# Permuted column orders for thirteen of the sixteen input tiles of a decoder step

## The chip, the cores and the metric

The kernel runs on one core of a Trainium2 chip. The metric is the device time of one execution in microseconds (us). Two versions of the kernel are told of here, before and after one change; what is known at this point is the time and the profile of the version before.

## The reference

One inference step of a one-layer decoder trunk, for a prompt of 256 positions and 8 sample rows that share the weights. With `rmsnorm` the root-mean-square norm over the 2048 channels, and cut to what carries the work:

```
h = h + 0.5 * swiglu_ffn(rmsnorm(h, g1), ffn1_w_gate, ffn1_w_up, ffn1_w_down)    # 2048 -> 5504 -> 2048
z = rmsnorm(h, gm) @ w_in                                                       # 2048 -> 10528 columns
zp, zr, zq, zg = split(z)          # pooling | RWKV-7 r,k,v and low-rank | queries | 3 gates of 2048
merged = sigmoid(zg0) * pool(zp) + sigmoid(zg1) * rwkv7(zr) + sigmoid(zg2) * attend(zq, memory)
h = h + merged @ w_o
h = h + 0.5 * swiglu_ffn(rmsnorm(h, g2), ffn2_w_gate, ffn2_w_up, ffn2_w_down)
y = rmsnorm(h, gf)
```

Beside `y` the step returns the memory keys and values and the new recurrent, shift and pooling states. Everything is float32.

## The kernel before, in words

All activations stand transposed in SBUF: channels on the 128 partitions, the 264 positions (256 of the prompt and 8 sample rows, `NT`) along the free dimension. A vector of 2048 channels is thus sixteen tiles of 128x264, numbered k = 0 to 15 (`KD` = 16).

Float32 products are made of three matmuls each in the type fp32r. Every weight tile and every activation tile is split into a high part and a low part (`whi`, `wlo` for weights, `x4h`, `x4l` for input tile 4), and `mm3` (lines 227 to 230) adds high times high (L228), low activation times high weight (L229) and high activation times low weight (L230) into one PSUM accumulator. In each of these matmuls the weight block of 128x128 is the stationary operand, and the activation tile of 128x264 is the moving operand, read column by column; the accumulator takes 264 columns.

`proj` (lines 232 to 241) makes one projection: it runs over the sixteen (or 8, or 43) activation tiles and issues `mm3` for each, so a projection from the normalised input is 48 matmuls in a row into one accumulator. Of the projections, 255 read the sixteen normalised input tiles `x0` to `x15`: 86 gates and ups in each of the two feed-forward blocks (the first pair of the first block is made by `first_tiles`, lines 442 to 462), and 83 column blocks of `w_in`. The others read the feed-forward's hidden tiles (`g0` to `g42`, the down projections), the merged branches (`mg`, for `w_o`) and the outputs of the branches.

Weights are streamed once. `nxt` and `emit_load` (lines 172 to 225) fetch 512 KB at a time by a DMA on SP's queue, ScalarE (ACT) rounds it to the high part (L182), VectorE (DVE) subtracts for the low part (L184), up to two loads ahead of the matmuls; a load serves 24 matmuls.

The input tiles are made at three places, each time into the same sixteen pairs of buffers: `x_tile` (lines 397 to 409) from the loaded input, `norm_tile` (lines 274 to 276) at the end of the first feed-forward block, and `norm_tile` again after `w_o`. `split_into` (lines 256 to 263) writes the high part by ACT (L261) and the low part by DVE (L262). Each buffer is 264 floats, 1,056 bytes a partition, and the 32 buffers lie one behind the other in the order x0h, x0l, x1h, x1l and so on. The start of an input tile therefore moves on by 2,112 bytes from k to k+1, and four tiles make 8,448 bytes, which is 33 times 256.

The order of the work is set by the program text and by the framework's scheduler, which arranges instructions of each engine once, when the program is built.

Of the kernel before, what the change touches and what calls it, by code (L numbers as in the profile page):

```python
# [10 lines left out]
F32R = mybir.dt.float32r  # L11
# [4 lines left out]
P = 128  # L16
# [3 lines left out]
NT = SEQ + NB  # L20
FF = 5504
NF = FF // P
KD = D // P
# [16 lines left out]
GATE_AHEAD = 3  # L40
FIRST = ((0, 2), (2, 4), (4, 8), (8, 12), (12, 16))
MEM_AT = 6
MEM_END = 8


@with_exitstack
def step_kernel(ctx: ExitStack, tc: tile.TileContext, I, O):
# [8 lines left out]
    xp = ctx.enter_context(tc.tile_pool(name="xp", bufs=1))  # L56
# [10 lines left out]
    def sb(pool, shape, tag, dt=F32, bufs=None):  # L67
        kw = {} if bufs is None else {"bufs": bufs}
        return pool.tile(shape, dt, tag=tag, name=nm(tag), **kw)
# [157 lines left out]
    def mm3(out, wh, wl, xh, xl, first, last):  # L227
        PE.matmul(out, lhsT=wh, rhs=xh, start=first, stop=False)  # L228
        PE.matmul(out, lhsT=wh, rhs=xl, start=False, stop=False)  # L229
        PE.matmul(out, lhsT=wl, rhs=xh, start=False, stop=last)  # L230

    def proj(name, nk, xs, m=P):
        acc = acc_tile()
        k = 0
        while k < nk:
            wh, wl, n = nxt(name)
            for j in range(n):
                xh, xl = xs[k]
                mm3(acc[:m, :NT], wh[:, j, :], wl[:, j, :], xh, xl, k == 0, k == nk - 1)
                k += 1  # L240
        return acc


    nstate = {}
# [5 lines left out]
    def split(dst_pool, src, tag, scale=None, shape=(P, NT)):  # L250
        hi = sb(dst_pool, list(shape), tag + "h", F32R)
        lo = sb(dst_pool, list(shape), tag + "l", F32R)
        split_into(hi, lo, src, scale)
        return hi, lo
# [17 lines left out]
            POOL.tensor_tensor(out=sq, in0=sq, in1=t, op=ALU.add)  # L272

    def norm_tile(ht, d, gcol):
        nstate["xs"].append(split(xp, ht, f"x{d}", gcol))
        sq_acc(ht, d)

    def refine(r, x, t):
# [60 lines left out]
    g1v = sb(cst, [P, 16], "g1v")  # L339
    p = ps()  # L340
# [15 lines left out]
    r, gi, off = 0, 0, 0  # L356
    for name, n in vrows:
        if name == "rwkv_mu":
            gi, r, off = 1, 0, gsz[0]
# [35 lines left out]
    h = []  # L395
    norm_begin()

    def x_tile(j):
        p = ps()
        for i in range(2):  # L400
            PE.transpose(p[:, i * P:(i + 1) * P], xv[i][:, j * P:(j + 1) * P], ident)
        PE.transpose(p[:, SEQ:NT], xsm[:, j * P:(j + 1) * P], ident[:NB, :NB])
        ht = sb(hp, [P, NT], f"h{j}")
        hi = sb(xp, [P, NT], f"x{j}h", F32R)
        lo = sb(xp, [P, NT], f"x{j}l", F32R)
        split_into(hi, lo, p[:, :NT], g1v[:, j:j + 1])
        (ACT.copy if j % 4 == 3 else DVE.tensor_copy)(out=ht, in_=p[:, :NT])
        nstate["xs"].append((hi, lo))
        h.append(ht)

    xsq = sb(st, [P, 11], "xsq")
# [32 lines left out]
    def first_tiles():  # L444
        x_tile(0)
        x_tile(1)
        accs = [acc_tile(), acc_tile()]
        state["look"] = 0
        for c, (k0, k1) in enumerate(FIRST):
            wh, wl, n = nxt(("ffn1", "gu", 0))  # L450
            if c + 1 < len(FIRST):
                x_load(c + 1)
            state["look"] = 1 if c + 1 < len(FIRST) else 2
            for k in range(k0, k1):
                if k + 2 < KD:
                    x_tile(k + 2)
                xh, xl = nstate["xs"][k]
                for q in range(2):
                    qs = slice(q * P, (q + 1) * P)
                    mm3(accs[q][:, :NT], wh[:, k - k0, qs], wl[:, k - k0, qs], xh, xl, k == 0, k == KD - 1)  # L460
            x_squares(c)
        return accs

# [118 lines left out]
    xs, rstd = nstate["xs"], sb(xp, [P, NT], "rstd")  # L582
# [13 lines left out]
    xs, rstd = norm_end()  # L596
# [41 lines left out]
    for g in range(4):  # L638
        w = WIN[g]
        acc = proj(("zp", g), KD, xs)  # L640
# [764 lines left out]
```

## Time and profile before

| | before |
|---|---|
| median of 3 runs | 2436.65 us (2435.9 to 2442.38) |
| the profiled execution | 2439.21 us, its span 2437.5 us |
| TensorE matmul busy | 2391.9 us, 98% of the span |
| VectorE, ScalarE, GpSimd busy | 60%, 45%, 21% |
| mean granted TensorE clock | 0.988 of full speed |

The span runs from the first to the last instruction; the profiled execution's own time is 1.7 us longer. [...] Where the granted clock is 1.00 TensorE runs at 2.4 GHz, where it is 0.50 at 1.2 GHz.

### The profile page before, as it was taken

The numbers are of one execution on the slowest core, as the hardware profiler recorded it, in microseconds if no ns is written. First come the engines' busy times: TensorE is split into PE (matmuls) and PEld (weight loads), VectorE is DVE, ScalarE is ACT, GpSimd is POOL, SyncE is SP. The second block draws the span as 40 slices with busy tenths as digits, with TensorE's granted clock in tenths as the row PEclk, the third lists the DMA queues.
The fourth block names the chain that finished last, engine by engine and source line by source line (L and its number), as shares of the span: only waits on it lengthen the run. The fifth ranks groups of instructions, "written<-read, shape, count | busy, mean of one in ns | idle before, by whom it ended". The sixth has DMA issues, their size and how long they took to land.

```text
span 2437.5 us, 47572 instructions
## 1 busy us (share of the span) xinstructions
PE 2391.9 (98%) x19703; PEld 2347.7 (96%) x19703; DVE 1452.6 (60%) x1828; ACT 1086.6 (45%) x1440; POOL 514.6 (21%) x594
## 2 busy tenths in 40 slices
PE   8999999999999998999989999999999999999998
PEld 8899999999999998899979999999999999999998
DVE  5655555555545559898895765566555555544444
ACT  6444444444444445564323744444444444444444
POOL 2211111211000026462381210111211112210000
PEclk9999999999999999999899999999999999999999
DMA  8576666666666877777755677776666666666664
GB/s 234 157 217 181 182 179 179 180 181 176 191 187 186 233 185 216 211 187 190 194 173 162 169 187 196 209 200 178 181 180 179 179 181 181 179 174 174 175 184 129
DMA packets 822460, 452.03 MB, mean 185 GB/s; under 512 B 29092, under 2 KB 806982, under 8 KB 821963
## 3 DMA queue, kind: packets, MB, share of 16 engines
q1 hardware_dynamic: 821795, 448.91, 65.9%
q8 instruction: 154, 2.52, 0.4%
q14 instruction: 63, 0.52, 0.1%
q0 software_dynamic: 448, 0.08, 0.0%
HBM read 430.19 MB, written 18.96 MB: 184 GB/s over the span
## 4 chain that ended last, share of the span: by engine, by line
PE 92%; DMA 2%; DVE 2%; issue 1%; POOL 1%; ACT 1%; SPq 0%; DVEq 0%; POOLq 0%; ACTq 0%
PE acc L228 29%; PE acc L230 29%; PE acc L229 28%; DMA qb<-qs_d 1%; DVE wlo L184 1%; POOL kc L746 1%; PE acc L517 1%; PE acc L518 1%; PE acc L519 1%; DMA c4k<-AR_d 1%; PE ps L917 0%; DMA raw<-in_ffn_w_up_dram 0%; PE ps L1075 0%; DVE c4k L994 0%; PE ps L1024 0%
## 5 line engine op out<-in xcount | busy, mean ns | idle before, releaser
L184 DVE TENSOR_TENSOR wlo<-raw,whi 128x1024 fp32r<-128x1024 f32 (+2 forms) x783 | 970.9, 1240 | 728.2 <-ACT whi L182 673.3
L182 ACT ACTIVATE whi<-raw 128x1024 fp32r<-128x1024 f32 (+2 forms) x783 | 809.8, 1034 | 1121.6 <-PE acc L229 732.4
L549 POOL TENSOR_TENSOR t<-t,rstd 128x264 f32<-128x264 f32 x86 | 123.3, 1434 | 860.6 <-ACT s L548 848.5
L272 POOL TENSOR_TENSOR sqs<-sqs,sqt 128x264 f32<-128x264 f32 x44 | 42.2, 958 | 546.3 <-ACT sqt L271 546.3
L230 PE MATMUL acc<-x0h,wlo 128*128 128x264 f32 (+1 forms) x255 | 73.3, 288 | 8.5 <-DVE wlo L184 4.6
L228 PE MATMUL acc<-x0h,whi 128*128 128x264 f32 (+1 forms) x255 | 77.5, 304 | 0.0
L228 PE MATMUL acc<-x8h,whi 128*128 128x264 f32 (+1 forms) x255 | 76.3, 300 | 0.0
L228 PE MATMUL acc<-x4h,whi 128*128 128x264 f32 (+1 forms) x255 | 74.0, 291 | 1.5 <-ACT x4h L261 1.5
L230 PE MATMUL acc<-x8h,wlo 128*128 128x264 f32 (+1 forms) x255 | 72.6, 285 | 2.5 <-DVE wlo L184 2.5
L552 DVE TENSOR_TENSOR g<-acc,s 128x264 f32<-128x264 f32 x86 | 37.2, 432 | 63.2 <-PE acc L230 61.0
L230 PE MATMUL acc<-x5h,wlo 128*128 128x264 f32 (+1 forms) x255 | 74.0, 290 | 0.0
L229 PE MATMUL acc<-x5l,whi 128*128 128x264 f32 (+1 forms) x255 | 73.9, 290 | 0.0
L230 PE MATMUL acc<-x13h,wlo 128*128 128x264 f32 (+1 forms) x255 | 73.9, 290 | 0.0
L229 PE MATMUL acc<-x2l,whi 128*128 128x264 f32 (+1 forms) x255 | 73.8, 289 | 0.0
L229 PE MATMUL acc<-x1l,whi 128*128 128x264 f32 (+1 forms) x255 | 73.7, 289 | 0.0
L230 PE MATMUL acc<-x1h,wlo 128*128 128x264 f32 (+1 forms) x255 | 73.7, 289 | 0.0
L230 PE MATMUL acc<-x9h,wlo 128*128 128x264 f32 (+1 forms) x255 | 73.6, 289 | 0.0
L228 PE MATMUL acc<-x11h,whi 128*128 128x264 f32 (+1 forms) x255 | 73.6, 289 | 0.0
L228 PE MATMUL acc<-x3h,whi 128*128 128x264 f32 (+1 forms) x255 | 73.5, 289 | 0.0
L229 PE MATMUL acc<-x13l,whi 128*128 128x264 f32 (+1 forms) x255 | 73.5, 288 | 0.0
L230 PE MATMUL acc<-x6h,wlo 128*128 128x264 f32 (+1 forms) x255 | 73.4, 288 | 0.0
L230 PE MATMUL acc<-x2h,wlo 128*128 128x264 f32 (+1 forms) x255 | 73.4, 288 | 0.0
(1172 smaller groups left out, 8826.0 us busy)
## 6 DMA issues: line engine op xcount, KB each, us to landing
raw<-in_ffn_w_gate_dram SPq DMA_DIRECT2D x170, 512.0 KB
raw<-in_ffn_w_up_dram SPq DMA_DIRECT2D x170, 512.0 KB
raw<-in_w_in_dram SPq DMA_DIRECT2D x164, 512.0 KB
raw<-in_ffn_w_down_dram SPq DMA_DIRECT2D x160, 512.0 KB
raw<-in_w_o_dram SPq DMA_DIRECT2D x32, 512.0 KB
raw<-in_rwkv_out_dram SPq DMA_DIRECT2D x16, 512.0 KB
raw<-in_ffn_w_down_dram SPq DMA_DIRECT2D x32, 192.0 KB
raw<-in_w_mem_k_dram SPq DMA_DIRECT2D x8, 512.0 KB
```

The lines of the kernel that those rows point to most:

```text
L182: ACT.activation(hi[:, :n * m], raw[:, :n * m], AF.Copy)
L184: DVE.tensor_tensor(out=lo[:, :n * m], in0=raw[:, :n * m], in1=hi[:, :n * m].bitcast(F32), op=ALU.subtract)
L228: PE.matmul(out, lhsT=wh, rhs=xh, start=first, stop=False)
L229: PE.matmul(out, lhsT=wh, rhs=xl, start=False, stop=False)
L230: PE.matmul(out, lhsT=wl, rhs=xh, start=False, stop=last)
L272: POOL.tensor_tensor(out=sq, in0=sq, in1=t, op=ALU.add)
L517: PE.matmul(accs[i], lhsT=xh, rhs=wh[:, j, :], start=k == 0, stop=False)
L518: PE.matmul(accs[i], lhsT=xh, rhs=wl[:, j, :], start=False, stop=False)
L519: PE.matmul(accs[i], lhsT=xl, rhs=wh[:, j, :], start=False, stop=k == 15)
L549: POOL.tensor_tensor(out=t1, in0=t1, in1=rstd, op=ALU.mult)
L552: DVE.tensor_tensor(out=g, in0=au[:, :NT], in1=s1, op=ALU.mult)
L746: POOL.tensor_tensor(out=kcs[b], in0=kcs[b], in1=qbs[b].unsqueeze(1).broadcast_to([P, 2, XW]), op=ALU.mult)
```

## The change

The program's instructions stay the same in number and order on every engine. What changes is in which order the columns of thirteen input tiles are read by the matmuls, and how those tiles lie in memory.

Each input tile k gets a layout of three numbers from the new table `XLAY`: R regions, a run q and a stride S in floats. The 264 columns are cut into R equal parts; part r is stored at an offset of r times S floats from the tile's start. `natural` names the columns in their own order (part after part), which is how ACT and DVE write a tile. `flow` names the same columns in the order in which the matmuls take them: q columns from the first part, q from the second, and so on round the R parts. The accumulator is addressed through the same permutation, so each column's sum lands where it did before. With `(1, 264, 264)` a tile is as before; tiles 0, 13 and 15 have that. Tile 7, `(2, 132, 136)`, has two parts with a gap of four floats between them and runs as long as a part, so its columns are still taken in their own order. The other twelve are taken in runs of 2, 4, 8, 12 or 44 columns from two, three or six regions.

Where S is larger than a part, the tile takes more room: tiles 2, 3, 5, 7, 9 and 14 grow by 32 to 96 bytes per buffer, so all tiles behind them, and the hidden tiles of the feed-forward blocks, begin at other addresses than before.

```diff
@@ -40,6 +40,8 @@
+XLAY = ((1, 264, 264), (2, 4, 132), (2, 4, 136), (2, 4, 144), (2, 12, 132), (2, 12, 136), (2, 44, 132), (2, 132, 136),
+        (3, 4, 88), (3, 4, 96), (3, 8, 88), (6, 4, 44), (2, 2, 132), (1, 264, 264), (2, 4, 140), (1, 264, 264))
@@ -236,9 +238,24 @@
-                mm3(acc[:m, :NT], wh[:, j, :], wl[:, j, :], xh, xl, k == 0, k == nk - 1)
+                out = flow(natural(acc[:m, :NT], k), k) if xs is nstate["xs"] else acc[:m, :NT]
+                mm3(out, wh[:, j, :], wl[:, j, :], xh, xl, k == 0, k == nk - 1)
                 k += 1
         return acc
+
+    def xtiles(k):
+        R, q, S = XLAY[k]
+        ts = [sb(xp, [P, max(NT, R * S)], f"x{k}{c}", F32R)[:, :R * S].rearrange("p (r s) -> p r s", r=R)[:, :, :NT // R]
+              for c in "hl"]
+        return ts
+
+    def flow(t, k):
+        R, q, S = XLAY[k]
+        return t if R == 1 else t.rearrange("p r (o q) -> p o r q", q=q)
+
+    def natural(t, k):
+        return t.rearrange("p (r x) -> p r x", r=XLAY[k][0])
@@ -272,7 +289,9 @@
     def norm_tile(ht, d, gcol):
-        nstate["xs"].append(split(xp, ht, f"x{d}", gcol))
+        hi, lo = xtiles(d)
+        split_into(hi, lo, natural(ht, d), gcol)
+        nstate["xs"].append((flow(hi, d), flow(lo, d)))
         sq_acc(ht, d)
```

`x_tile` and `first_tiles` are changed in the same way.

On TensorE the rows of one projection of the mixer stage stood so before, with 264 columns as the last number of each (the names are the accumulator, the input tile and the weight tile):

```order
L228 MATMUL acc_9604<-x3h_7375,whi_9515 128x264
L229 MATMUL acc_9604<-x3l_7376,whi_9515 128x264
L230 MATMUL acc_9604<-x3h_7375,wlo_9517 128x264
L228 MATMUL acc_9604<-x4h_7550,whi_9515 128x264
L229 MATMUL acc_9604<-x4l_7551,whi_9515 128x264
L230 MATMUL acc_9604<-x4h_7550,wlo_9517 128x264
```

The same rows after the change, with the accumulator's pattern as runs, regions and columns of a run:

```order
L230 MATMUL acc_9604<-x3h_7375,whi_9515 128x33x2x4
L231 MATMUL acc_9604<-x3l_7376,whi_9515 128x33x2x4
L232 MATMUL acc_9604<-x3h_7375,wlo_9517 128x33x2x4
L230 MATMUL acc_9604<-x4h_7550,whi_9515 128x11x2x12
L231 MATMUL acc_9604<-x4l_7551,whi_9515 128x11x2x12
L232 MATMUL acc_9604<-x4h_7550,wlo_9517 128x11x2x12
```

Nothing has moved in the sequence; the lines are two further down in the file, and the 264 columns have become 33 rounds of 2 regions of 4 columns for tile 3, and 11 rounds of 2 regions of 12 for tile 4.

## Rows read from the trace of the kernel before

**Rows 1.** The page: busy time by engine, and the chain that ended last.

```profile
PE 2391.9 (98%) x19703; PEld 2347.7 (96%) x19703; DVE 1452.6 (60%) x1828; ACT 1086.6 (45%) x1440; POOL 514.6 (21%) x594
...
PE 92%; DMA 2%; DVE 2%; issue 1%; POOL 1%; ACT 1%; SPq 0%; DVEq 0%; POOLq 0%; ACTq 0%
PE acc L228 29%; PE acc L230 29%; PE acc L229 28%; DMA qb<-qs_d 1%; DVE wlo L184 1%; POOL kc L746 1%; PE acc L517 1%; PE acc L518 1%; PE acc L519 1%; DMA c4k<-AR_d 1%; PE ps L917 0%; DMA raw<-in_ffn_w_up_dram 0%; PE ps L1075 0%; DVE c4k L994 0%; PE ps L1024 0%
```

**Rows 2.** Busy time in one stretch of the first feed-forward block.

```profile
core 0: us, PE busy (x) PEld busy (x) DVE busy (x) ACT busy (x) POOL busy (x), PEclk, DMA share, GB/s
250.00:600.00 350.00, 350.00 (x2867) 350.00 (x2866) 180.59 (x206) 144.67 (x179) 64.99 (x58) 1.00 0.64 179
```

**Rows 3.** Timeline of TensorE, four input tiles: start us, duration us, instruction.

```profile
1501.24 0.29 PE L228 MATMUL acc<-x4h,whi 128*128 128x264 f32 x1
1501.37 0.28 PE L229 MATMUL acc<-x4l,whi 128*128 128x264 f32 x1
1501.48 0.28 PE L230 MATMUL acc<-x4h,wlo 128*128 128x264 f32 x1
1501.60 0.28 PE L228 MATMUL acc<-x5h,whi 128*128 128x264 f32 x1
...
1502.71 0.29 PE L228 MATMUL acc<-x8h,whi 128*128 128x264 f32 x1
```

**Rows 4.** Line 229 by tile: duration in ns, least, median, most.

```profile
L229 PE MATMUL acc<-x4l,whi x255: 279/279/587, 18.2 to 2164.6; 128*128 128x264 f32 x127, 128*32 128x264 f32 x1
...
L229 PE MATMUL acc<-x5l,whi x255: 279/287/588, 20.4 to 2164.9; 128*128 128x264 f32 x127, 128*32 128x264 f32 x1
...
L229 PE MATMUL acc<-x6l,whi x255: 279/284/588, 22.7 to 2165.3; 128*128 128x264 f32 x127, 128*32 128x264 f32 x1
...
L229 PE MATMUL acc<-x7l,whi x255: 280/282/480, 24.8 to 2165.7; 128*128 128x264 f32 x127, 128*32 128x264 f32 x1
...
L229 PE MATMUL acc<-x8l,whi x255: 279/279/422, 26.1 to 2166.0; 128*128 128x264 f32 x127, 128*32 128x264 f32 x1
```

**Rows 5.** Busy time and granted clock in a stretch at half clock.

```profile
1200.60:1201.90 1.30, 1.30 (x7) 1.30 (x7) 0.43 (x1) 0.78 (x1) 0.00 (x0) 0.50 0.82 230
```

**Rows 6.** Timeline of TensorE in that stretch, the first and the sixth matmul.

```profile
1200.62 0.42 PE L229 MATMUL acc<-x15l,whi 128*128 128x264 f32 x1
...
1201.71 0.41 PE L228 MATMUL acc<-oh,whi 128*128 128x264 f32 x1
```

**Rows 7.** Timeline of TensorE, matmuls of 512 columns, the first and the ninth.

```profile
134.80 0.40 PE L518 MATMUL acc<-wlo,m5h 128*128 128x512 f32 x1
...
136.67 0.40 PE L517 MATMUL acc<-whi,m7h 128*128 128x512 f32 x1
```

**Rows 8.** Timeline of TensorE, weight blocks of 32 columns, first and thirteenth.

```profile
900.66 0.29 PE L228 MATMUL acc<-x9h,whi 128*32 128x264 f32 x1
...
902.12 0.29 PE L228 MATMUL acc<-x13h,whi 128*32 128x264 f32 x1
```

**Rows 9.** Line 261, the high part of an input tile: ns, least, median, most.

```profile
L261 ACT ACTIVATE x1h<-h,vec x2: 501/510/518, 616.5 to 1582.8; 128x264 fp32r<-128x264 f32 x2
```

**Rows 10.** Line 262, the low parts of three neighbouring input tiles.

```profile
L262 DVE SCALAR_TENSOR_TENSOR x1l<-h,vec,x1h x2: 987/992/996, 617.5 to 1584.1; 128x264 fp32r<-128x264 f32 x2
L262 DVE SCALAR_TENSOR_TENSOR x2l<-h,vec,x2h x2: 983/994/1004, 633.2 to 1590.0; 128x264 fp32r<-128x264 f32 x2
L262 DVE SCALAR_TENSOR_TENSOR x3l<-h,vec,x3h x2: 994/1003/1012, 648.8 to 1595.8; 128x264 fp32r<-128x264 f32 x2
```

**Rows 11.** The page: the costliest groups, the rounding and splitting of the weights.

```profile
L184 DVE TENSOR_TENSOR wlo<-raw,whi 128x1024 fp32r<-128x1024 f32 (+2 forms) x783 | 970.9, 1240 | 728.2 <-ACT whi L182 673.3
L182 ACT ACTIVATE whi<-raw 128x1024 fp32r<-128x1024 f32 (+2 forms) x783 | 809.8, 1034 | 1121.6 <-PE acc L229 732.4
```

More of the change, by code (lines that the diff above doesn't have):

```diff
@@ L403, in x_tile @@
         ht = sb(hp, [P, NT], f"h{j}")
-        hi = sb(xp, [P, NT], f"x{j}h", F32R)
-        lo = sb(xp, [P, NT], f"x{j}l", F32R)
-        split_into(hi, lo, p[:, :NT], g1v[:, j:j + 1])
+        hi, lo = xtiles(j)
+        split_into(hi, lo, natural(p[:, :NT], j), g1v[:, j:j + 1])
         (ACT.copy if j % 4 == 3 else DVE.tensor_copy)(out=ht, in_=p[:, :NT])
-        nstate["xs"].append((hi, lo))
+        nstate["xs"].append((flow(hi, j), flow(lo, j)))
         h.append(ht)
@@ L459, in first_tiles @@
                     qs = slice(q * P, (q + 1) * P)
-                    mm3(accs[q][:, :NT], wh[:, k - k0, qs], wl[:, k - k0, qs], xh, xl, k == 0, k == KD - 1)
+                    mm3(flow(natural(accs[q][:, :NT], k), k), wh[:, k - k0, qs], wl[:, k - k0, qs], xh, xl, k == 0,
+                        k == KD - 1)
             x_squares(c)
```

## The prediction, made before the change was timed

> **What bounds the kernel now.** I read the page first, then the busy times of a dense stretch, then TensorE's timeline there and at three places where one thing differs. The page leaves no doubt about the engine: the matmuls are busy for 98% of the span, the chain that ended last runs through TensorE for 92% of it, and three lines, those of `mm3`, hold 86% [rows 1]. Whatever one matmul of these lines costs is paid some 17,000 times (86% of 2437.5 us at the 122 ns found below), and the other engines have room: a load of weights serves 24 matmuls, about 2.9 us, and takes 1.24 us of DVE and 1.03 us of ACT [rows 11].
>
> What one matmul costs is the spacing of starts. In a dense stretch 2867 matmuls fill 350 us at full clock, 122.1 ns each [rows 2]. The columns alone would need 264 / 2.4 GHz = 110.0 ns. So about 12 ns, a tenth, goes to something else. Three comparisons say where that tenth belongs.
>
> First, it follows the tile. Twelve matmuls on tiles 4 to 7 take 1502.71 - 1501.24 = 1.47 us, so 122 ns on the mean, but the single spacings are 0.13, 0.11 and 0.12 us in the first three [rows 3]; and the low part's matmul has a median of 279 ns on tile 4, 287 on tile 5, 284 on 6, 282 on 7, and again 279 on tile 8 [rows 4]. The period is four tiles, and four tiles are 33 times 256 bytes: the cost depends on where in a 256-byte stretch of SBUF the reading begins. Second, it goes away at half clock: there the spacing is (1201.71 - 1200.62) / 5 = 0.218 us at a granted clock of 0.50 [rows 5, 6], and 264 / 1.2 GHz = 0.220. Third, it grows with the columns read: matmuls of 512 columns stand (136.67 - 134.80) / 8 = 233.8 ns apart [rows 7], 20.5 ns over 512 / 2.4 GHz = 213.3. Between 264 and 512 columns the slope is (233.8 - 122.1) / 248 = 0.450 ns a column in place of 0.417, so of the 12.1 ns some 0.0337 x 264 = 8.9 ns go with the columns and 3.2 ns are fixed per matmul.
>
> It doesn't seem to be the weights. Where the weight blocks have 32 columns instead of 128, twelve matmuls on tiles 9 to 12 still take 902.12 - 900.66 = 1.46 us [rows 8]. So the 8.9 ns belong to the fast reading of the moving tile, or to the writing of its columns, and that is what the change reorders.
>
> [...]
>
> **The change part by part.** No instruction is added or moved on any engine, and SP's and POOL's queues hold what they held. Three things change.
>
> 1. *The making of the tiles.* ACT's and DVE's splits write the same 264 columns in two or three pieces where the stride is larger than the part. They are 13 x 3 x 2 = 78 instructions of 0.51 us on ACT [rows 9] and 0.99 us on DVE [rows 10], off the chain: 15.7 us lie between two of them at the end of the first feed-forward block and 5.9 us after `w_o` (starts 617.5, 633.2 and 1584.1, 1590.0 in [rows 10]). I cost this at nothing. If a split took half as long again, DVE's 0.5 us would still lie beside matmuls, except after the last tile of each of the three makings, and tile 15 is unchanged.
>
> 2. *The addresses.* Six tiles grow, so the starts of the tiles behind them shift inside the 256 bytes. The four kinds of start differ by 8 ns in a single matmul [rows 4], but sums over a period of four tiles are 1.47 and 1.46 us [rows 3, 8], so shifting starts trades one kind for another. The difference of 0.01 in 1.47 us, 0.7% of the 2096 us that the three lines hold, bounds it at 14 us either way; I take nothing.
>
> 3. *The order of reading and of writing the sums.* 255 projections of three matmuls read each tile, 765 matmuls per tile. Tile 7 keeps its order, so 12 x 765 = 9,180 matmuls are reordered. No row of before shows a matmul with such an order, so this is bounded from both sides. Below: all of the 8.9 ns goes, 9,180 x 8.9 ns = 82 us less. Above: every change of region costs time. One round trip needs 66 changes for a run of 4, 22 for 12, 6 for 44, 33 for 8 and 132 for 2; over the twelve tiles these are 677 per projection and line, times 765 = 518,000 in all. If each cost one column time, 0.417 ns, the kernel would lose 216 us; if reading in pieces went at the half-clock pace of [rows 6], 9,180 x (218 - 122) ns = 881 us.
>
> I take a value near the lower end, because of how the excess looks. A cost that depends on the start inside 256 bytes and recurs with the length read is that of a pass: 264 columns are 1,056 bytes, 4.1 passes through such a stretch, at 8.9 / 4.1 = 2.2 ns a pass. Two regions in turn pass through it at half the pace each. If something else is met once per pass, a slower pass that has once been pushed aside stays aside longer. So I let the six tiles with two regions and runs of 4 or 12 (1 to 5 and 14) lose half of the 8.9 ns, and leave the tiles with three or six regions, with runs of 44 and of 2 as they are: 6 x 765 x 4.45 ns = 20.4 us.
>
> The sum: 2439.2 us of the profiled execution - 20.4 = 2418.8 us. The median of the runs stands 2.6 us lower than that execution, so 2436.65 - 20.4 = 2416 us is forecast. Faster matmuls would ask for weights sooner; at 179 GB/s and a DMA share of 0.64 [rows 2] a matmul shorter by 2% finds them.
>
> **The rivals.**
>
> *All of it goes.* If the reading in pieces avoids the meeting altogether on all twelve tiles: 2436.65 - 82 = 2355 us. For it speaks only that the excess is bound to the order of addresses; against it that the twelve layouts differ so much that they can hardly all be right.
>
> *Nothing that the order reaches.* If the excess comes from the array's or the accumulator's side or at a fixed rate in time, any order pays it: 2437 us, within the 7 us that a measurement of this kernel can't tell from no change (0.3%). For it speaks that the sum over four tiles is nearly the same for weights of 128 and of 32 columns and for any alignment; against it that the single spacings follow the address so closely.
>
> *The regions get in each other's way.* The regions of a tile are offset by 16 to 176 bytes within the 256, and a run that jumps back can meet what its partner just left. If the jumps double the excess on the twelve tiles, 82 us are added: 2519 us. It decides from the point where the added cost of a change of region passes 20.4 us / 518,000 = 0.04 ns, a tenth of a column time; that is very little, and this is what makes it strong. For it speaks that one tile in natural order already loses a tenth to addresses alone. If each change costs a full column time, it is 2653 us.
>
> [...]
>
> **How the numbers follow.** Partial relief, 2395 to 2429 us: 0.31, the likeliest, with 2416 us. More than that, below 2395: 0.11. No effect, 2429 to 2444: 0.18. Regions in each other's way, 2444 to 2545: 0.26; above that, with a column time a change or the half-clock pace: 0.14. So faster by over 0.3% has 0.42, within 0.3% 0.18, slower 0.40. The range that leaves out 0.2 goes from 2370, which leaves out a twentieth, to 2545, which leaves out 0.14.
>
> **What would show it.** The spacing of starts by tile in the timeline of the changed kernel decides everything. Right: tiles 1 to 5 and 14 near 117 to 118 ns, the others at 120 to 124, tiles 0, 13 and 15 as before. Wrong towards no effect: every period of four tiles still takes 1.46 to 1.47 us. Wrong towards slower: spacings that grow with the number of changes, tile 12 (132 changes) and tiles 1, 2, 3, 8, 9, 11 (66) above tiles 4, 5, 10 and 6, which would be a price per change; or spacings that sort by stride and not by run, which would be a meeting of regions. Splits off the chain stay so if TensorE's busy share stays at 98%.

## The result, and the profile after

| | before | after |
|---|---|---|
| median of the runs | 2436.28 us (2434.84 to 2442.38, 4 runs) | 2518.57 us (2514.68 to 2520.19, 4 runs) |
| span of the profiled execution | 2437.5 us | 2518.5 us |
| TensorE matmul busy | 2391.9 us | 2478.6 us |
| mean granted TensorE clock | 0.988 | 0.991 |

The ratio is 1.0333, with a 95% interval of 1.0316 to 1.035: the change makes the kernel 3.3% slower. The forecast was 2416 us and had the sign wrong. The time falls on the number that the rival "The regions get in each other's way" gave, 2519 us, but by luck: not for the reason that this number was worked out from, as will be seen.

The page of the changed kernel answers to [rows 1]. The lines of `mm3` are now 230 to 232.

```profile
PE 2478.6 (98%) x19703; PEld 2433.4 (97%) x19703; DVE 1450.2 (58%) x1828; ACT 1088.5 (43%) x1440; POOL 514.9 (20%) x594
...
PE 93%; DMA 2%; DVE 2%; issue 1%; POOL 1%; ACT 1%; SPq 0%; DVEq 0%; POOLq 0%; ACTq 0%
PE acc L230 29%; PE acc L232 29%; PE acc L231 29%; DVE wlo L186 1%; POOL kc L765 1%; DMA qb<-qs_d 1%; PE acc L536 1%; PE acc L538 1%; PE acc L537 1%; PE ps L936 0%; DMA c4k<-AR_d 0%; DMA raw<-in_ffn_w_up_dram 0%; DVE c4k L1175 0%; PE ps L1222 0%; PE ps L1052 0%
```

The bound is the same, the same 19,703 matmuls are only longer. The dense stretch of [rows 2] says by how much:

```profile
250.00:600.00 350.00, 350.00 (x2700) 350.00 (x2699) 172.36 (x197) 136.61 (x169) 62.81 (x56) 1.00 0.61 170
```

2700 matmuls in 350 us at full clock are 129.6 ns each, where it was 122.1. Times 12,240 matmuls (255 projections, 48 each) this is 92 us. The span grew by 81: TensorE's idle time fell from 2437.5 - 2391.9 = 45.6 us to 39.9, and the time at half clock fell from about 2 x 0.012 x 2437.5 = 58 us to 45, an estimate from the mean clocks of 0.988 and 0.991 that takes 0.50, the clock of [rows 5], as the only one below full; this by itself gives back some 6.6 us of matmuls.

Which tiles? The timeline of the changed kernel (start us, duration us, instruction; the durations, 0.29 to 0.34 us, are longer than the distances of the starts, 0.13 to 0.17, so matmuls overlap in it), first around tile 12, then from tile 4 to tile 9:

```profile
1333.49 0.34 PE L230 MATMUL acc<-x12h,whi 128*128 128x264 f32 x1
1333.66 0.34 PE L231 MATMUL acc<-x12l,whi 128*128 128x264 f32 x1
1333.83 0.34 PE L232 MATMUL acc<-x12h,wlo 128*128 128x264 f32 x1
1334.00 0.29 PE L230 MATMUL acc<-x13h,whi 128*128 128x264 f32 x1
...
1576.15 0.29 PE L230 MATMUL acc<-x4h,whi 128*128 128x264 f32 x1
...
1576.54 0.29 PE L230 MATMUL acc<-x5h,whi 128*128 128x264 f32 x1
...
1577.66 0.32 PE L230 MATMUL acc<-x8h,whi 128*128 128x264 f32 x1
1577.80 0.33 PE L231 MATMUL acc<-x8l,whi 128*128 128x264 f32 x1
1577.96 0.33 PE L232 MATMUL acc<-x8h,wlo 128*128 128x264 f32 x1
1578.12 0.29 PE L230 MATMUL acc<-x9h,whi 128*128 128x264 f32 x1
```

Three matmuls on tile 12 take 0.51 us, on tile 8 0.46, on tile 4 0.39; in [rows 3] twelve took 1.47, so three took 0.37. The medians of the low part's line show the same, against 279, 287 and 279 ns for tiles 4, 5 and 8 in [rows 4] and 279 for tile 12. Tile 12's line before, then four of after:

```profile
L229 PE MATMUL acc<-x12l,whi x255: 279/279/422, 33.0 to 2167.5; 128*128 128x264 f32 x127, 128*32 128x264 f32 x1
```

```profile
L231 PE MATMUL acc<-x4l,whi x255: 287/293/589, 18.0 to 2245.2; 128*128 128x264 f32 x127, 128*32 128x264 f32 x1
L231 PE MATMUL acc<-x5l,whi x255: 290/292/589, 20.3 to 2245.6; 128*128 128x264 f32 x127, 128*32 128x264 f32 x1
...
L231 PE MATMUL acc<-x8l,whi x255: 322/330/412, 25.8 to 2246.8; 128*128 128x264 f32 x127, 128*32 128x264 f32 x1
...
L231 PE MATMUL acc<-x12l,whi x255: 338/343/428, 33.0 to 2248.4; 128*128 128x264 f32 x127, 128*32 128x264 f32 x1
```

From here on I give one number per tile, its *spacing*: the distance from the start of each of its matmuls to the next start on TensorE, taken from the trace, without those over 200 ns (half clock, waits), averaged over all projections and the three lines. The first matmul behind a dear tile (one with a large spacing) is slower: on tile 13, behind tile 12, the first of the three lines has 131.3 ns in place of 122.4 before, on tile 9, behind tile 8, 132.5 in place of 122.3. On these two tiles the other two lines fell instead, and the mean stayed.

| tile | layout (regions, run, stride) | before ns | after ns |
|---|---|---|---|
| 1, 2, 3, 14 | two regions, runs of 4 | 123.7, 121.9, 122.0, 121.9 | 130.0, 127.5, 125.9, 125.8 |
| 4, 5 | two regions, runs of 12 | 120.8, 123.9 | 128.0, 127.1 |
| 6 | (2, 44, 132) | 122.0 | 123.7 |
| 8 | (3, 4, 88) | 120.8 | **154.8** |
| 9 | (3, 4, 96) | 123.9 | 124.1 |
| 10, 11 | (3, 8, 88), (6, 4, 44) | 122.1, 122.0 | 124.0, 124.1 |
| 12 | (2, 2, 132) | 120.7 | **168.3** |
| 0, 7, 13, 15 | columns in their own order | 120.8, 122.0, 124.0, 122.1 | 122.9, 122.3, 123.8, 122.8 |

Two tiles hold (34.0 + 47.6) x 765 = 62 of the 92 us. Tiles 8 and 9 differ only in the distance of the regions, 88 or 96 floats.

At half clock the same orders cost nothing that shows. One stretch of the changed kernel at a granted clock of 0.50 (busy times, clock), and its timeline, which answer to [rows 5, 6]:

```profile
1321.60:1322.70 1.10, 1.10 (x7) 1.10 (x7) 0.31 (x1) 0.00 (x0) 1.10 (x1) 0.50 0.94 247
```

```profile
1321.57 0.42 PE L230 MATMUL acc<-x12h,whi 128*128 128x264 f32 x1
1321.79 0.42 PE L231 MATMUL acc<-x12l,whi 128*128 128x264 f32 x1
1322.01 0.42 PE L232 MATMUL acc<-x12h,wlo 128*128 128x264 f32 x1
1322.23 0.42 PE L230 MATMUL acc<-x13h,whi 128*128 128x264 f32 x1
```

Tile 12 stands 0.22 us apart, as the plain order does in [rows 6] with 0.218. No matmul on tile 8 fell into half clock in this run, but its layout, (3, 4, 88), did as tile 9 of the sweep of run lengths below:

```profile
1013.10:1014.00 0.90, 0.90 (x6) 0.90 (x6) 0.90 (x3) 0.00 (x0) 0.90 (x1) 0.50 1.06 296
```

```profile
1013.04 0.42 PE L230 MATMUL acc<-x9l,whi 128*128 128x264 f32 x1
1013.26 0.42 PE L231 MATMUL acc<-x9h,wlo 128*128 128x264 f32 x1
1013.48 0.42 PE L229 MATMUL acc<-x10h,whi 128*128 128x264 f32 x1
```

Again 0.22 us. So 168 ns is not a fixed number of TensorE's cycles, which would be 336 ns there. It looks as if something with a speed of its own can't follow at full clock; no run shows what.

The splits answer to [rows 9, 10]. ACT's line for one tile, then DVE's (ns: least, median, most):

```profile
L278 ACT ACTIVATE x3h<-h,vec x2: 502/510/517, 677.8 to 1644.6; 128x264 fp32r<-128x264 f32 x2
```

```profile
L279 DVE SCALAR_TENSOR_TENSOR x3l<-h,vec,x3h x2: 984/996/1008, 678.8 to 1645.9; 128x264 fp32r<-128x264 f32 x2
```

510 and 996 ns, against 510 and 1003 before: writing a tile in two parts costs nothing that shows. Tile 9, in three parts, has 508 and 996 ns, before 508 and 994.

### The profile page after: what moved, and what is told of

It reads as the page before. It is cut to its first block, busy times and chain, and to the rows that moved or that the text cites. A ratio compares the mean times of both kernels' runs of the same rounds, so it can differ in the third digit from the quotient of the medians.

```text
span 2518.5 us, 47566 instructions
## 1 busy us (share of the span) xinstructions
PE 2478.6 (98%) x19703; PEld 2433.4 (97%) x19703; DVE 1450.2 (58%) x1828; ACT 1088.5 (43%) x1440; POOL 514.9 (20%) x594
## 4 chain that ended last, share of the span: by engine, by line
PE 93%; DMA 2%; DVE 2%; issue 1%; POOL 1%; ACT 1%; SPq 0%; DVEq 0%; POOLq 0%; ACTq 0%
PE acc L230 29%; PE acc L232 29%; PE acc L231 29%; DVE wlo L186 1%; POOL kc L765 1%; DMA qb<-qs_d 1%; PE acc L536 1%; PE acc L538 1%; PE acc L537 1%; PE ps L936 0%; DMA c4k<-AR_d 0%; DMA raw<-in_ffn_w_up_dram 0%; DVE c4k L1175 0%; PE ps L1222 0%; PE ps L1052 0%
## 5 line engine op out<-in xcount | busy, mean ns | idle before, releaser
L568 POOL TENSOR_TENSOR t<-t,rstd 128x264 f32<-128x264 f32 x86 | 123.9, 1440 | 920.3 <-ACT s L567 920.3
L232 PE MATMUL acc<-x12h,wlo 128*128 128x264 f32 (+1 forms) x255 | 88.0, 345 | 0.0
L231 PE MATMUL acc<-x12l,whi 128*128 128x264 f32 (+1 forms) x255 | 87.7, 344 | 0.0
L230 PE MATMUL acc<-x12h,whi 128*128 128x264 f32 (+1 forms) x255 | 85.4, 335 | 0.0
L231 PE MATMUL acc<-x8l,whi 128*128 128x264 f32 (+1 forms) x255 | 84.1, 330 | 0.0
L565 DVE TENSOR_TENSOR t<-acc,rstd 128x264 f32<-128x264 f32 x86 | 37.2, 433 | 76.4 <-PE acc L232 76.4
L230 PE MATMUL acc<-x2h,whi 128*128 128x264 f32 (+1 forms) x255 | 75.8, 298 | 0.0
L230 PE MATMUL acc<-x13h,whi 128*128 128x264 f32 (+1 forms) x255 | 75.7, 297 | 0.0
L231 PE MATMUL acc<-x4l,whi 128*128 128x264 f32 (+1 forms) x255 | 75.7, 297 | 0.0
L230 PE MATMUL acc<-x1h,whi 128*128 128x264 f32 (+1 forms) x255 | 75.5, 296 | 0.0
L232 PE MATMUL acc<-x4h,wlo 128*128 128x264 f32 (+1 forms) x255 | 75.4, 296 | 0.0
```

What stands on the lines that cost most here:

```text
L565: DVE.tensor_tensor(out=t1, in0=ag[:, :NT], in1=rstd, op=ALU.mult)
L568: POOL.tensor_tensor(out=t1, in0=t1, in1=rstd, op=ALU.mult)
```

## The experiments

**Two layouts, or a price for every change of region?** The table of the change with two entries put back:

```diff
-        (3, 4, 88), (3, 4, 96), (3, 8, 88), (6, 4, 44), (2, 2, 132), (1, 264, 264), (2, 4, 140), (1, 264, 264))
+        (1, 264, 264), (3, 4, 96), (3, 8, 88), (6, 4, 44), (1, 264, 264), (1, 264, 264), (2, 4, 140), (1, 264, 264))
```

> Tiles 8 and 12 are read in natural order again, the other eleven permuted tiles stay. Theory A (the loss sits in two layouts, three regions 88 floats apart in runs of 4, and two regions 132 apart in runs of 2): tile 8 falls from 154.8 to about 122 ns, tile 12 from 168.3 to about 122 ns, 765 x (33 + 46) ns = 61 us less than the changed kernel, about 2457 us, still some 20 us above the kernel before. Theory B (a price per change of region, the same for every tile: 82 us over 677 changes): the two tiles hold 198 of the 677 changes, 24 us less, about 2495 us.

Measured: 2462.89 us (2459.16 to 2463.69), ratio to before 1.0105 (1.008 to 1.013). Theory A; B's 2495 is out. Tile 12 is back at 121.7 ns, tile 8 only at 126.7, which is 3.6 of the 6 us above 2457: a plain tile, too, depends on its place. The line by tile:

```profile
L230 PE MATMUL acc<-x8l,whi x255: 281/298/425, 24.8 to 2189.6; 128*128 128x264 f32 x127, 128*32 128x264 f32 x1
...
L230 PE MATMUL acc<-x12l,whi x255: 282/285/422, 31.8 to 2191.1; 128*128 128x264 f32 x127, 128*32 128x264 f32 x1
```

**Reading, writing, or addresses?** Three kernels take the change apart.

```diff
+    def straight(t, k):   # regions and runs in the order of the memory
+        R, q, S = XLAY[k]
+        return t if R == 1 else t.rearrange("p (o r q) -> p o r q", r=R, q=q)
# read only: the accumulator is straight
-                out = flow(natural(acc[:m, :NT], k), k) if xs is nstate["xs"] else acc[:m, :NT]
+                out = straight(acc[:m, :NT], k) if xs is nstate["xs"] else acc[:m, :NT]
# write only: tiles are plain 264 columns and read straight
-        nstate["xs"].append((flow(hi, d), flow(lo, d)))
+        nstate["xs"].append((straight(hi, d), straight(lo, d)))
# padding only: runs as long as a part, as (2, 132, 144) or (3, 88, 96)
```

> The input tiles are read in the permuted orders of the change, but the sums are written to the accumulator in consecutive columns, so the columns of those products are scrambled. Theory A (the cost is on the reading of SBUF): tile 8 stays near 155 ns, tile 12 near 168 ns, tiles 1 to 5 and 14 stay 3 to 7 ns above their old spacing, the time stays near 2518 us. [...]

> The input tiles lie and are read in consecutive columns as before the change; only the accumulator is addressed in the permuted orders, so the columns of those products are scrambled. Theory A (reading of SBUF): every tile at 121 to 124 ns, time near 2437 us. Theory B (writing of PSUM): tile 8 near 155 ns, tile 12 near 168 ns, time near 2518 us. If runs of 2 cost on the writing side and three regions on the reading side, tile 12 stays near 168 ns here and tile 8 falls to 122 ns: about 2473 us.

> The tiles have the strides, gaps and addresses of the change, but the columns are read and written part after part, in their own order. Theory A (the order costs, not the addresses): all tiles between 120 and 125 ns, time 2437 us within 7 us. Theory B (the shifted addresses or the gaps cost): tiles 8 and 12 or their neighbours keep part of the loss; the time stays over 2450 us.

Measured, one run each: read only 2519.69 us, write only 2445.11, padding only 2439.23, beside 2436.82 before. First the dense stretch and tile 12's low part of read only:

```profile
250.00:600.00 350.00, 350.00 (x2700) 350.00 (x2699) 171.95 (x198) 137.81 (x170) 62.65 (x56) 1.00 0.60 170
```

```profile
L231 PE MATMUL acc<-x12l,whi x255: 338/343/428, 32.6 to 2247.9; 128*128 128x264 f32 x127, 128*32 128x264 f32 x1
```

Then the same two of write only:

```profile
250.00:600.00 350.00, 350.00 (x2860) 350.00 (x2859) 179.97 (x206) 143.99 (x179) 65.02 (x58) 1.00 0.64 179
```

```profile
L231 PE MATMUL acc<-x12l,whi x255: 279/287/422, 31.9 to 2173.4; 128*128 128x264 f32 x127, 128*32 128x264 f32 x1
```

And the dense stretch of padding only:

```profile
250.00:600.00 350.00, 350.00 (x2868) 350.00 (x2867) 180.79 (x206) 144.93 (x179) 64.90 (x58) 1.00 0.64 179
```

Reading alone has the same 2700 matmuls in the stretch as the change, and every tile's spacing is the changed kernel's within 0.2 ns. Writing alone has 2860, 122.4 ns each, padding alone 2868 against 2867 before. So the loss lies in the order in which SBUF is read. By the sum of spacings, writing alone is worth 3 us and padding alone less than 1, though single tiles move by up to 3.5 ns with their addresses.

So writing the sums in pieces, with runs down to two columns, takes 122.4 ns a matmul in place of 122.1; its single run is 8 us above before.

**A sweep of distances, and the same layouts at all places.** The table alone is changed (in the first of these kernels, in the second one of the next sweep and in those that read a few places over and over, the raw weight buffers are four in place of five, to make room):

```diff
+XLAY = ((3, 4, 88), (3, 4, 92), ..., (3, 4, 116), (2, 2, 132), (2, 2, 136), ..., (2, 2, 160))
# and, in another kernel
+XLAY = ((3, 4, 88),) * 8 + ((2, 2, 132),) * 8
```

> Sixteen layouts in one kernel, read tile by tile: tiles 0 to 7 have three regions in runs of 4, 88, 92, 96, 100, 104, 108, 112 and 116 floats apart; tiles 8 to 15 two regions in runs of 2, 132, 136, 140, 144, 148, 152, 156 and 160 apart. The raw weight buffers are four in place of five, to make room. Theory A (runs of 4, a whole 16 bytes, cost only where the distance is wrong; runs of 2 cost at any distance, since each takes half of 16 bytes): tiles 0 to 7 differ, 88 near 155 ns, 96 near 124 ns; tiles 8 to 15 all at 160 to 170 ns. Theory B (the distance decides for both): the tiles with runs of 2 differ too, some of them under 130 ns. Theory C (three regions cost about 155 ns and 96 is the exception): seven of the first eight near 155 ns.

> The two dear layouts alone: tiles 0 to 7 three regions 88 apart in runs of 4, tiles 8 to 15 two regions 132 apart in runs of 2, no padding, so each layout stands at eight tile starts. Theory A (the layout is dear wherever it stands): every one of tiles 0 to 7 at 145 to 165 ns, every one of 8 to 15 at 160 to 175 ns; in all 8 x 765 x (33 + 46) ns = 483 us more than the kernel before, about 2920 us. Theory B (the start inside 256 bytes or the neighbours decide): the eight tiles of a layout spread over more than 15 ns, some near 125 ns, and the time is well under 2900 us.

Measured: three regions in runs of 4 at 88, 92, 96 and so on to 116 floats: 155.4, 130.2, 125.8, 120.2, 123.3, 121.3, 121.7, 127.8 ns. Two regions in runs of 2: 169.4 to 170.9 at seven distances, 177.7 at the eighth. That is theory A, whose 160 to 170 ns for runs of 2 are passed at the last distance. Some of the tiles, by the low part's line:

```profile
L230 PE MATMUL acc<-x0l,whi x255: 322/324/422, 8.1 to 2463.3; 128*128 128x264 f32 x127, 128*32 128x264 f32 x1
...
L230 PE MATMUL acc<-x3l,whi x255: 278/284/422, 13.5 to 2464.5; 128*128 128x264 f32 x127, 128*32 128x264 f32 x1
...
L230 PE MATMUL acc<-x13l,whi x255: 337/339/420, 36.2 to 2468.9; 128*128 128x264 f32 x127, 128*32 128x264 f32 x1
```

The two dear layouts, at eight places each: 153.7 to 154.0 ns and 169.4 to 170.7, 2883.3 us in all. The place and the neighbours don't matter for them.

**A sweep of run lengths, and of what is whole and what is cut.**

```diff
+XLAY = ((2, 12, 132), (2, 2, 132), (2, 4, 132), (2, 6, 132), (2, 44, 132), (2, 22, 132), (2, 66, 132), (2, 132, 132),
+        (3, 2, 88), (3, 4, 88), (3, 8, 88), (3, 22, 88), (3, 44, 88), (3, 88, 88), (1, 264, 264), (1, 264, 264))
```

> Run lengths at one distance: tiles 0 to 7 have two regions 132 floats apart in runs of 12, 2, 4, 6, 44, 22, 66 and 132; tiles 8 to 13 three regions 88 apart in runs of 2, 4, 8, 22, 44 and 88; tiles 14 and 15 are plain. Theory A (16 bytes are one visit, and a visit takes 168.3 / 132 = 1.275 ns where that is more than the columns' own time): runs of 2 near 168 ns with two and with three regions; runs of 6, which make 88 visits or 112 ns, and of 22 and 66 stay at 120 to 130 ns. Theory B (a price per change of region, 46 ns / 132 = 0.35 ns): runs of 6 with 44 changes near 137 ns, runs of 12 and 22 near 126 to 130 ns, and runs of 2 in three regions near 168 ns. Runs of 4 in three regions: again near 155 ns by a theory of their distance, near 145 by the price per change (66 changes).

> Tiles 0 to 15, as regions, run, distance in floats: (2,4,134) (2,6,134) (2,6,136) (2,12,134) (4,2,66) (4,6,66) (6,2,44) (6,4,44) (11,4,24) (11,8,24) (22,4,12) (33,4,8) (22,6,12) (3,4,90) (3,4,120) and plain. Theory A (whole, aligned 16 bytes are cheap however many regions there are, and anything that cuts 16 bytes is dear): (6,4,44), (11,4,24), (11,8,24), (22,4,12), (33,4,8) and (3,4,120) at 119 to 133 ns; runs of 2 near 170 ns or above; runs of 6 near 158 ns at any distance; (2,4,134) and (2,12,134), whose second region starts 8 bytes off, between 130 and 155 ns. Theory B (a price per change of region or per region): (33,4,8), (22,4,12) and (11,4,24) above (6,4,44), and (2,4,134) like (2,4,132). Theory C (distance decides): no order by run length, single layouts among those with whole 16 bytes over 140 ns.

Measured in the first: runs of 2 170.7 ns (two regions) and 198 (three; the median at full clock, since the limit of 200 ns would cut into this tile); runs of 6 158.0; of 22 133.6; of 4 131.1, of 12 129.7, of 66 126.9, of 44 126.7. Three regions: runs of 4 160.8, of 8 126.1, of 22 131.0, of 44 124.3. Both theories miss: a price per change gave 137 ns for runs of 6, a price per visit of 16 bytes 120 to 130, and for runs of 2 in three regions both gave 168. Runs of 6 in two regions, then of 2 and of 8 in three, by the low part's line:

```profile
L230 PE MATMUL acc<-x3l,whi x255: 329/336/421, 13.5 to 2331.0; 128*128 128x264 f32 x127, 128*32 128x264 f32 x1
...
L230 PE MATMUL acc<-x8l,whi x255: 367/374/455, 25.0 to 2333.0; 128*128 128x264 f32 x127, 128*32 128x264 f32 x1
...
L230 PE MATMUL acc<-x10l,whi x255: 281/290/422, 28.1 to 2334.0; 128*128 128x264 f32 x127, 128*32 128x264 f32 x1
```

In the second, where the distance is at times not a multiple of 4 floats:

| layout | spacing ns | |
|---|---|---|
| (22, 4, 12), (33, 4, 8), (3, 4, 120) | 119.6, 120.6, 123.3 | whole 16 bytes |
| (11, 8, 24), (6, 4, 44) | 126.6, 131.9 | whole, behind dear tiles |
| (11, 4, 24) | 160.9 | whole |
| (2, 12, 134), (2, 4, 134), (3, 4, 90) | 149.1, 175.1, 157.2 | second region 8 bytes off |
| (2, 6, 134), (2, 6, 136), (4, 6, 66), (22, 6, 12) | 162.4, 159.1, 175.9, 157.7 | runs of 6 |
| (6, 2, 44), (4, 2, 66) | 239.8, 261.0 | runs of 2 (mean of all below 320 ns) |

```profile
L230 PE MATMUL acc<-x4l,whi x255: 411/443/521, 17.4 to 2564.7; 128*128 128x264 f32 x127, 128*32 128x264 f32 x1
...
L230 PE MATMUL acc<-x8l,whi x255: 330/336/422, 24.2 to 2567.0; 128*128 128x264 f32 x127, 128*32 128x264 f32 x1
L230 PE MATMUL acc<-x9l,whi x255: 283/283/390, 25.7 to 2567.5; 128*128 128x264 f32 x127, 128*32 128x264 f32 x1
L230 PE MATMUL acc<-x10l,whi x255: 277/282/385, 27.0 to 2567.9; 128*128 128x264 f32 x127, 128*32 128x264 f32 x1
L230 PE MATMUL acc<-x11l,whi x255: 280/282/388, 31.9 to 2568.2; 128*128 128x264 f32 x127, 128*32 128x264 f32 x1
```

Here x4 is (4, 2, 66), x8 (11, 4, 24), x9 (11, 8, 24), x10 (22, 4, 12) and x11 (33, 4, 8). Theory A holds in kind but for one layout, though (2, 4, 134) and (4, 6, 66), with 175 and 176 ns, are dearer than the 130 to 155 and the 158 that it gave: all that often cuts 16 bytes is dear (149 to 261 ns), and 22 or 33 regions in whole 16 bytes, with 66 changes each, are no dearer (119.6 and 120.6 ns) than the plain order (122.1). That ends a price per change. The exception, (11, 4, 24), has regions 24 floats apart, and 88 = 64 + 24: the two dear layouts in whole 16 bytes share a distance of 96 bytes modulo 256. The distance is not enough by itself: in runs of 8 the same two distances take 126.1 and 126.6 ns.

**A few places over and over.** If 96 bytes were a clash of two places, two places would do. In these kernels the tiles are plain, and a product reads only some columns of them, again and again:

```diff
     def flow(t, k):
...
+        if R == 1:
+            return t[:, 0, :q].unsqueeze(1).broadcast_to([P, NT // q, q])
+        v = t[:, 0, :2 * S] if R == 2 else t[:, 0, :3 * S]
+        v = v.rearrange("p (r s) -> p r s", r=R)[:, :, :q]
+        return v.unsqueeze(1).broadcast_to([P, NT // (R * q), R, q])
```

> No regions here. Tiles 0, 2, 4, 6 and 15 plain; tiles 1, 3 and 5 in natural order but beginning 8, 16 and 24 bytes behind the tile's start; tiles 7 to 14 read only their first 4, 8, 12, 24, 44, 66, 88 and 132 columns, over and over until 264 columns are read (so those products leave out the rest of the tile). Theory A (the tenth above the columns' own 110 ns is in the reading of SBUF, at places that recur with the addresses): reading the same 16 or 32 bytes falls to 110 to 115 ns or leaves the 122 ns far in the other direction. Theory B (the tenth does not come from where SBUF is read): all repeats at 120 to 125 ns. Starts: if four columns are fetched as 16 bytes that must begin at a multiple of 16, tiles 1 and 5 straddle at every step and go to 160 to 175 ns as runs of 2 do, tile 3 stays; if only the order of places counts, all three stay at 120 to 126 ns.

> No layouts: every tile is stored plain, and each product reads only two runs of 4 columns, the first at the tile's start and the second d floats behind it, in turn until 264 columns are read (the rest of the tile is left out); d is 4, 8, 12 and so on to 64 floats for tiles 0 to 15. Theory A (two places whose distance is 24 floats, 96 bytes, modulo 64 floats, 256 bytes, are dear one after the other; that is what 88 floats in three regions and 24 floats in eleven have in common, and 96 to 120 lack): d = 24 at 140 to 160 ns, 20 and 28 perhaps 5 to 10 ns up, all others at 112 to 123 ns. Theory B (two places alone never are; it takes a walk through many places): all sixteen at 112 to 123 ns.

> Sixteen cases; in all but tiles 7 to 10 a product reads only a few places over and over (regions, run, distance): (1,2) (2,2,4) (2,2,132) (2,2,8) (2,2,6) (1,6) (2,6,132), then as layouts (2,2,132) (2,4,152) (3,4,152) and plain, then over and over (3,4,88) (3,4,24) (2,4,88) (2,4,132) (2,2,64). Theory A for runs of 2 (the time goes by the number of runs of 8 bytes that don't follow on, wherever they are): (2,2,4), (2,2,132), (2,2,8), (2,2,6) and (2,2,64) all near 170 ns; a price by place would leave some of them at 112 to 123 ns. Theory A for runs of 4 (96 bytes modulo 256): layout (3,4,152) near 154 ns and (2,4,152) over 131 ns; over and over, (3,4,88), (3,4,24) and (2,4,88) over 140 ns, (2,4,132) near 113 ns. Theory B (it takes a walk through many places): the last five all at 112 to 123 ns, the layout (3,4,152) still dear.

Measured. The first 4, 8 and 12 columns over and over: 113.0, 113.6 and 113.5 ns, as theory A had it; 24 columns 120.6; 44 to 132 columns 121.4 to 127.2. Plain order, beginning 8, 16 or 24 bytes later: 126.3, 120.8, 123.0, so the guess of 160 to 175 ns for starts off 16 bytes fell. Pairs of places: 112.3 to 114.2 ns at all sixteen distances, 112.4 at 24 floats, so theory A fell. Two runs of 2 over and over: 113.7 to 114.6 at all five distances; one run of 2 or of 6 over and over: 113.8 and 112.7. Theory A fell again, while the layout (2, 2, 132) stands at 171.0 in the same kernel. The layout (3, 4, 152), whose 152 is 88 + 64, takes 152.1 ns, as 96 bytes modulo 256 have it, but (2, 4, 152) only 129.3, behind a dear tile, and (3, 4, 88) and (3, 4, 24) over and over take 113.6, (2, 4, 88) and (2, 4, 132) 113.4 and 112.7. Only two runs of 6, (2, 6, 132), are dear even there, 156.1 ns. A dense stretch with pairs alone, then three tiles of the third kernel (runs of 6 over and over, the layout (3, 4, 152), (3, 4, 88) over and over):

```profile
250.00:600.00 350.00, 350.00 (x3076) 350.00 (x3075) 193.68 (x219) 155.57 (x191) 62.34 (x58) 1.00 0.69 194
```

```profile
L230 PE MATMUL acc<-x6l,whi x255: 314/321/423, 20.2 to 2178.6; 128*128 128x264 f32 x127, 128*32 128x264 f32 x1
...
L230 PE MATMUL acc<-x9l,whi x255: 323/329/413, 24.7 to 2180.0; 128*128 128x264 f32 x127, 128*32 128x264 f32 x1
...
L230 PE MATMUL acc<-x11l,whi x255: 274/278/428, 29.7 to 2180.8; 128*128 128x264 f32 x127, 128*32 128x264 f32 x1
```

So, but for the two runs of 6, neither a jump nor a pair of places is dear in itself (112 to 115 ns); it takes a walk through more places. And the tenth above the columns' own 110 ns (an estimate: half of the 0.22 us that 264 columns take at half clock) is of the same kind: all but 3 ns of it are gone where at most three places of 16 bytes are read. The other engines and the DMAs are not its source by themselves: in the stretch with pairs alone they are busier than in [rows 2] (VectorE 193.68 us in place of 180.59, 194 GB/s in place of 179), and a matmul takes 113.8 ns.

**A clash of more places?** Two runs of 12 columns over and over, at sixteen distances:

```diff
+XLAY = tuple((2, 12, 4 * s, 1) for s in range(3, 19))
```

> No layouts: each product reads only two runs of 12 columns (48 bytes, three times 16), the second s times 16 bytes behind the first, in turn until 264 columns are read; s is 3 to 18 for tiles 0 to 15. Theory A (a clash of places: with runs of 6 and 528 bytes between them, a repeat of only 12 columns took 157 ns; what clashes are places a fixed power of two apart, read at the same time for different rows of the array): most s at 112 to 122 ns, and a group of neighbouring s (those that bring two of the six places to the same 16 bytes modulo 64, 128 or 256) over 130 ns. Theory B (only runs that cut 16 bytes, like 6, are dear in a repeat): all sixteen at 112 to 122 ns.

Measured: 120.7 to 126.7 ns for all sixteen, no group stands out. Both theories miss: a clash at a fixed distance shows nowhere, and six places of 16 bytes already pay the tenth or more, as the 24 columns above did (120.6).

**Does the order set the tenth too?** The one layout that was quiet in all three lines, every third 16 bytes in three passes, put on the kernel before, and the same on every operand of `proj`; then every second 16 bytes:

```diff
+    def third(t, r=22):
+        return t.rearrange("p (r o q) -> p o r q", r=r, q=4)
-                mm3(acc[:m, :NT], wh[:, j, :], wl[:, j, :], xh, xl, k == 0, k == nk - 1)
+                mm3(third(acc[:m, :NT]), wh[:, j, :], wl[:, j, :], third(xh), third(xl), k == 0, k == nk - 1)
```

> The kernel before, with all sixteen input tiles read and summed in runs of 4 columns from 22 places 12 floats apart (every third 16 bytes, three passes), tiles stored as before, no padding. Theory A (what is dear or cheap is the walk through the addresses; this one gave 119.6 ns in all three lines where one tile had it): 12,240 matmuls x (122.1 - 119.6) ns = 31 us less than before, about 2406 us. Theory B (the 119.6 ns was the place of that one tile or its neighbours): 2436 us within 7 us. Theory C (a price per change of region, 66 a matmul): over 2500 us.

> As f1_third_unit_inputs, and the hidden tiles of the feed-forward blocks, the merged branches and all others that these projections read are taken in the same order: about 17,000 matmuls. Theory A: 17,000 x 2.5 ns = 43 us less than before, about 2394 us, and under f1_third_unit_inputs by some 12 us. Theory B: 2436 us within 7 us.

> As f2_third_unit_all, but 33 places 8 floats apart (every second 16 bytes, two passes). One tile with this layout gave 118.3 to 122.5 ns in the three lines, 120.6 on the mean. Theory A: 17,000 x 1.5 ns = 26 us less than before, about 2411 us. Theory B (no gain without the place of that tile): 2436 us within 7 us.

Measured: input tiles 2409.19 us, ratio 0.9881 (0.9864 to 0.9898); all operands 2398.67 us, 0.9836 (0.9819 to 0.9853); every second 16 bytes 2428.69 us, 0.9956 (0.9942 to 0.9971). The first two come within 5 us of theory A, the third gives a third of it. The gain depends on the place: in the first kernel twelve tiles are at 118.1 to 119.0 ns, but tiles 0, 4, 8 and 12, which begin alike modulo 256 bytes, stay at 121.7 to 122.1. The dense stretch of the second, and its low part by tile:

```profile
250.00:600.00 350.00, 350.00 (x2932) 350.00 (x2931) 184.23 (x211) 147.83 (x182) 62.83 (x56) 1.00 0.66 184
```

```profile
L229 PE MATMUL acc<-x4l,whi x255: 278/288/425, 18.0 to 2130.8; 128*128 128x264 f32 x127, 128*32 128x264 f32 x1
L229 PE MATMUL acc<-x5l,whi x255: 277/280/588, 19.9 to 2131.1; 128*128 128x264 f32 x127, 128*32 128x264 f32 x1
```

2932 matmuls are 119.4 ns each. This version beats both kernels, by 1.6% the one before: an order of reading can take a fifth of the 12 ns away, only not the orders of this change.

## Why the prediction was wrong

**The bound and the place of the excess** were right. TensorE's matmuls set the time before and after, and most of the tenth above 110 ns comes from the fast reading of the moving tile: it falls from 12 to 3 ns when few places are read, which fits the 3.2 ns that the prediction called fixed, and it depends on the order. The 2.4 GHz behind the 110 ns agrees with the rows: 264 columns in 0.218 us at a granted clock of 0.50 [rows 5, 6] are 1.21 columns a ns, and twice that at 1.00, an estimate, gives 109 ns. The count of 255 x 3 matmuls per tile was right with it.

**The splits at nothing** were right: 510 and 996 ns after. **The addresses at nothing**, within 14 us, too: padding alone gave 2439.23 us against 2436.82.

**The step that failed** is the third part's choice: "Two regions in turn pass through it at half the pace each", from which six tiles were to lose half of their 8.9 ns and the others nothing. The six went up by 6.3, 5.6, 3.9, 7.2, 3.2 and 3.9 ns instead, 23 us in the sum of spacings in place of -20.4. Its premise, that the excess is a price per pass through 256 bytes, doesn't hold either: 24 columns, 96 bytes, read over and over take 120.6 ns. The larger mistake is the choice's second half, to "leave the tiles with three or six regions, with runs of 44 and of 2 as they are". For tiles 6, 9, 10 and 11 that held (0.2 to 2.1 ns). For tile 8 it was 34.0 ns and for tile 12 47.6 ns off, 62 us. The model had one idea, the pace of a pass through 256 bytes, and so no term at all for a cut of 16 bytes and none for the distance of regions. The choice lay near the lower bound, -82 us, with upper ones at +216 and +881 us and no row that spoke for its sign; medians that differ by 8 ns by address alone could have been read as a warning that an order may cost as well as gain.

**The rivals.** "The regions get in each other's way" came out at 2519 us because it doubled the excess on twelve tiles. The sum fits by luck, the mechanism doesn't: by it each of them would be at about 131 ns, and the twelve stand from 123.7 to 168.3. Its decision by a price per change is refuted by 66 changes at 119.6 ns and 66 at 154. "All of it goes" and "Nothing that the order reaches" are both out for these layouts; but that order reaches the tenth is shown from the other side by the 2398.67 us. Writing the sums in pieces costs 3 us by the spacings and 8 by its one time here, far from the +881 us of the half-clock bound.

**What would show it** had the right test, spacings by tile. They sort neither by run alone nor by stride alone: tile 12 by its run, whatever the stride; tile 8 by its stride, at the same run as tile 9.

**What stays open.** Why a walk through regions 96 bytes apart modulo 256 is dear in runs of 4 with three or eleven regions, while two regions, runs of 8, or two or three places over and over, at that distance aren't; and why cut runs are dear in a walk, and two runs of 6 even in a repeat. That nothing of it is left at half clock (0.22 us for tile 12 and for the plain order) would fit a supply from SBUF that all but keeps up with the full clock in the plain order, but that is a guess: no run measured that supply by itself. The two layouts that would test it, at 240 and 261 ns over the 220 of half clock, met no half clock in their run.

## What to carry to other kernels

Where TensorE bounds a kernel, look at the spacing of starts per tile and compare it with what the columns alone take, here an estimated 110 ns, half of the 0.22 us at half clock; 9 of the 12 ns between them went when few places were read, and 2.7 with a better order. In this kernel layouts that often cut 16 bytes (runs of 2 or 6, starts 8 bytes off) took 149 to 261 ns; those of whole, aligned pieces of 16 bytes took 118 to 132, but in runs of 4 at distances of 24, 88 and 152 floats 152 to 161. So make a permuted order of float32 columns of whole, aligned pieces first, and try its distances on the chip one tile at a time: a table with sixteen layouts in one kernel gives sixteen answers in one run. When a change mixes many variants, bound the worst of them singly: here two of twelve held 62 of the 92 us, though the other ten alone still lost 1.05%.

## What the runs showed of the hardware

- Reading 2 to 12 columns over and over, 264 columns take 113 to 114 ns; 24 or more, or the plain tile, take 120 to 127.
- A moving tile read in runs of 2 float32 columns takes 170 ns from two regions, 198 from three, 240 from six and 261 from four. At half clock two regions take 220, as the plain order does.
- Three regions 88 or 152 floats apart, or eleven 24 apart, in runs of 4 take 152 to 161 ns; three 92 to 120 apart 120 to 130; in runs of 8, 88 or 24 apart, 124 to 127.
- Accumulators written in runs of 2 to 44 columns cost 0.3 ns a matmul in a dense stretch (122.4 ns against 122.1, one run).
- Every third 16 bytes in three passes is faster than one pass in order: 119.4 ns against 122.1.
